# A mixer's first 60 microseconds: dt made token by token, two half projections ahead of the last norm tiles, identity transposes and a table load while inputs arrive

## The chip, the cores and the metric

The kernel runs on one core of a Trainium2 chip. A core has TensorE (PE, the matrix multiplier; its weight loads are shown apart as PEld), VectorE (DVE), ScalarE (ACT), GpSimd (POOL), a SyncE queue (SP) that issues DMAs, and on-chip memories: SBUF for operands, PSUM for what PE writes. The metric is device time in microseconds. The kernel before takes 2033.29 us (median of three executions, 2032.45 to 2035.05).

## The reference

The block reads 512 frames and 16 meta tokens of width 1024. It normalises every row, projects it to many columns, runs a chunked state-space scan and a short convolution, merges both, and ends with a large expert layer. Only its first part is touched by the change:

```python
h = jnp.concatenate([pad, meta, x], axis=1)
u = rmsnorm(h, ln_mix[l]) * valid
proj = u @ w_in[l]
z, xs, bs, cs, dt, sb, sc, sx, gates = jnp.split(proj, split_idx, axis=-1)
...
xbc = jax.nn.silu(causal_dwconv(xbc, conv_w) + conv_b) * valid
dt = jax.nn.softplus(dt.astype(jnp.float32) + dt_bias)      # 32 columns, one per head
a = -jnp.exp(a_log.astype(jnp.float32))
y = ssd_chunked_scan(xh * dtg[..., None], dtg * a, bs, cs)  # needs a running sum of dt * a
```

The width of `dt` is 32, one number per head and token. Every other slice of the projection is a multiple of 128 wide.

## The kernel before

**Number format.** Every matrix product that matters is made of three passes on PE: each operand is split into a rounded high part and the rest (`whi`, `wlo` of a weight; `uh`, `ul` of the normalised rows), and high x high, high x low and low x high are summed in PSUM. A weight block of 128 x 1024 is loaded by an SP DMA into `raw`, rounded by ACT into `whi` (L156), and DVE subtracts to get `wlo` (L157). A `Stream` object does this one block ahead of use; it has four `raw` buffers and three of each of `whi` and `wlo`.

**The norm.** Five tiles of rows enter: the 16 meta rows (`xm`) and four tiles of 128 frames (`xin`). They are handled in two groups, tiles 0 to 2 and tiles 3 and 4. Of each group ACT squares and sums the rows (L172; DVE for the 16 rows, L170), DVE computes the reciprocal root by three Newton steps (L128 to L133) and scales the rows into `xn` (L178). PE then transposes each tile, eight blocks of 128 columns in two PSUM banks (L187, tile `tps`); ACT rounds them into `uh` (L189) and DVE subtracts into `ul` (L190). From then on tokens run along the free axis: `uh` and `ul` hold 528 tokens.

**The projections.** `ft` (L224) makes one block of 128 output columns for all 528 tokens: 8 blocks of the inner dimension, 3 passes each, in two halves of 264 tokens, which is 48 passes with 264 moving columns (L233, tile `pj`, two PSUM buffers). The first block holds `dt`; it is called with `split=True`, so its first half (24 passes) needs the tokens of tiles 0 to 2 alone and stands ahead of the transposes of tiles 3 and 4. ACT copies the 32 useful rows out (L240), PE transposes them back to tokens-by-heads (L243, L245, tile `dtps`), and DVE and ACT make softplus from that (L246 to L266, `adt` at the end). Then come the blocks of group 0: `xs` twice, `bT` and `cT` by `ft`, each followed by a convolution and silu on ACT and DVE, then `zs` (tile `pz`).

**The running sums.** When `adt` is there, PE makes the running sums (L270 to L274: `meps`, `acps`, `atps`), short passes of 32 moving columns with a fixed 128 x 128 matrix on either side. They are in plain fp32, which costs two passes for each product. I call these 34 passes the burst. The scan of group 0 needs them.

**What sets the order.** The code is given to a scheduler that fixes the order of instructions on each engine when the kernel is built; on the chip every engine then runs its own list strictly in that order, and waits at an instruction until its inputs are there. After the first 60 us PE has a list of products up to the end of the kernel, with the other engines beside it.

## Time and profile before

| what | value |
|---|---|
| median of the runs | 2033.29 us |
| profiled execution | 2032.79 us, its span 2031.1 us |
| PE busy | 2001.7 us, 99% of the span |
| DVE, ACT, POOL busy | 1470.3, 914.8, 528.3 us |
| chain that ended last | PE 91%, DVE 6%, DMA 1%, ACT 1%, issue 1% |
| mean granted clock of TensorE | 0.997 of full speed |

A line of the timeline reads: start in us from the span's beginning, duration, engine, line of the kernel, operation, output<-inputs, shapes, count, and in brackets the idle time before it and who ended that. Consecutive instructions of one kind stand on one line with their count. A PE row's duration holds the time that a pass needs to run through the array, so the distance from one start to the next is what a pass costs in a dense row. [...]

### The profile page before, as it was taken

The page shows a single profiled execution, that of the slowest core. Times are in us where ns is not written, and L with a number is a line of the kernel's source. Part 1 is how long each engine was busy: PE and PEld are TensorE (multiplying, and loading weights), DVE is VectorE, ACT ScalarE, POOL GpSimd, SP SyncE. Part 2 cuts the span into 40 slices and gives each one's busy share as a digit, 9 for nine tenths or more (in the row PEclk, how much of TensorE's full clock was granted, in tenths as well). Part 3 has the DMA queues.
Part 4 walks back from the last instruction along what each step waited for, and adds up shares of the span by engine and source line. Part 5 has one row for each costly group of instructions (what it writes and reads, how often), then busy time and mean ns, then how long its engine had stood idle before and what let it go on. Part 6 is the DMA issues. An engine that isn't in the chain of part 4 may idle for free.

```text
span 2031.1 us, 31082 instructions
## 1 busy us (share of the span) xinstructions
PE 2001.7 (99%) x11944; PEld 1821.4 (90%) x11944; DVE 1470.3 (72%) x2705; ACT 914.8 (45%) x1281; POOL 528.3 (26%) x435
## 2 busy tenths in 40 slices
PE   7999999999999999999999999999999999999997
PEld 6999999999888888889999999999999998888886
DVE  6577777764322236479787879698988888988887
ACT  4877777732222223333447588433333332333333
POOL 1222222200000000331000000467555555633330
PEclk9999999999999999999999999999999999999999
DMA  4322323222222234224556667999999999999992
GB/s 150 121 95 89 100 87 96 84 74 94 94 94 94 96 112 166 73 84 143 183 178 219 244 242 275 372 396 397 396 396 353 359 352 334 392 380 382 385 379 101
DMA packets 175844, 439.57 MB, mean 216 GB/s; under 512 B 13776, under 2 KB 81584, under 8 KB 175568
## 3 DMA queue, kind: packets, MB, share of 16 engines
q1 hardware_dynamic: 135088, 290.62, 41.1%
q0 software_dynamic: 40320, 145.40, 19.3%
q8 instruction: 93, 1.52, 0.3%
q10 hardware_dynamic: 288, 1.57, 0.2%
q14 instruction: 55, 0.45, 0.1%
HBM read 395.53 MB, written 42.01 MB: 215 GB/s over the span
## 4 chain that ended last, share of the span: by engine, by line
PE 91%; DVE 6%; DMA 1%; ACT 1%; issue 1%; SPq 0%; POOL 0%; ACTq 0%; DVEq 0%; POOLq 0%
PE pj L233 13%; PE vps L137 8%; PE vps L136 8%; PE vps L138 8%; PE sps L136 7%; PE sps L137 7%; PE sps L138 7%; PE f L137 2%; PE f L136 2%; PE f L138 2%; PE gps L834 2%; PE pz L137 1%; PE pz L138 1%; PE pz L136 1%; PE qps L137 1%; PE qps L138 1%
## 5 line engine op out<-in xcount | busy, mean ns | idle before, releaser
L156 ACT CAST whi<-raw 128x1024 fp32r<-128x1024 f32 x393 | 411.9, 1050 | 811.9 <-issue 189.9
L157 DVE TENSOR_TENSOR wlo<-raw,whi 128x1024 fp32r<-128x1024 f32 x374 | 459.5, 1230 | 299.6 <-ACT whi L156 286.8
L136 PE MATMUL sps<-u2h,whi 128*128 128x384 f32 x1024 | 344.4, 336 | 0.0
L138 PE MATMUL sps<-u2h,wlo 128*128 128x384 f32 x1024 | 343.4, 335 | 0.3
L137 PE MATMUL sps<-u2l,whi 128*128 128x384 f32 x1024 | 342.9, 335 | 0.0
L137 PE MATMUL vps<-wlo,wh 128*128 128x512 f32 x768 | 299.3, 390 | 0.8 <-DVE wlo L157 0.8
L136 PE MATMUL vps<-whi,wh 128*128 128x512 f32 x768 | 299.0, 389 | 0.0
L138 PE MATMUL vps<-whi,wl 128*128 128x512 f32 x768 | 298.9, 389 | 0.0
L894 POOL DMA_INDIRECT row<-v,eix x128 | 180.1, 1407 | 213.6 <-DVE acc L906 194.4
L894 POOL DMA_INDIRECT row<-u,eix x128 | 190.9, 1491 | 131.1 <-DVE row L904 94.2
L136 PEld LDWEIGHTS sps<-u2h,whi 128*128 128x128 f32 x1024 | 192.3, 188 | 1.9
L137 PEld LDWEIGHTS sps<-u2l,whi 128*128 128x128 f32 x1024 | 192.3, 188 | 1.9
L138 PEld LDWEIGHTS sps<-u2h,wlo 128*128 128x128 f32 x1024 | 192.2, 188 | 1.6 <-DVE wlo L157 1.6
L138 PEld LDWEIGHTS vps<-whi,wl 128*128 128x128 f32 x768 | 144.1, 188 | 30.1
L137 PEld LDWEIGHTS vps<-wlo,wh 128*128 128x128 f32 x768 | 144.2, 188 | 29.5 <-DVE wlo L157 1.5
L136 PEld LDWEIGHTS vps<-whi,wh 128*128 128x128 f32 x768 | 144.1, 188 | 28.7 <-ACT whi L156 0.5
L233 PE MATMUL pj<-uh,whi 128*128 128x264 f32 (+1 forms) x784 | 165.4, 291 | 0.2 <-ACT uh L189 0.2
L906 DVE SCALAR_TENSOR_TENSOR acc<-row,sdot,acc 128x1024 f32<-128x1024 f32 x128 | 163.9, 1281 | 0.9
L233 PE MATMUL pj<-ul,whi 128*128 128x264 f32 (+1 forms) x784 | 162.2, 286 | 0.3 <-DVE ul L190 0.2
L233 PE MATMUL pj<-uh,wlo 128*128 128x264 f32 (+1 forms) x784 | 162.3, 286 | 0.0
L904 DVE SCALAR_TENSOR_TENSOR row<-row,u2t 128x1024 f32<-128x1024 f32 x128 | 151.3, 1220 | 12.3 <-DMA row<-u,eix 12.2
L999 ACT CAST wh<-wt 128x768 fp32r<-128x768 f32 x64 | 53.6, 838 | 163.2 <-PE vps L137 139.8
(286 smaller groups left out, 3610.5 us busy)
## 6 DMA issues: line engine op xcount, KB each, us to landing
raw<-u_t SPq DMA_DIRECT2D x128, 512.0 KB, 5.2
raw<-v SPq DMA_DIRECT2D x128, 512.0 KB, 12.3
raw<-w_a SPq DMA_DIRECT2D x73, 512.0 KB, 3.5
gsc<-gst SPq DMA_DIRECT2D x48, 512.0 KB, 4.4
gt<-gsc SPq DMA_DIRECT2D x32, 768.0 KB, 16.2
raw<-w_b SPq DMA_DIRECT2D x40, 512.0 KB, 3.4
asc<-so SPq DMA_DIRECT2D x36, 384.0 KB, 2.6
raw<-asc SPq DMA_DIRECT2D x36, 384.0 KB, 10.8
```

Of the source, the lines that this page charges most:

```text
L136: PE.matmul(ps, lh, rh, start=start, stop=False)
L137: PE.matmul(ps, lh, rl, start=False, stop=False)
L138: return PE.matmul(ps, ll, rh, start=False, stop=stop)
L156: A.copy(hi, r)
L157: self.last = self.lo(i).tensor_tensor(lo, r, hi.bitcast(F32), op=OP.subtract)
L233: PE.matmul(ps[:, hf, :w], w_[:, ks], u_[:, k, off + hf * w:off + (hf + 1) * w], start=(k == 0 and q == 0), stop=(k == KD - 1 and q == 2))
L834: PE.matmul(ps[:, i], oi[:, j, 1], og[:, j, x], start=x == 0, stop=x == 1)
L894: PL.indirect_dma_start(out=row, out_offset=None, in_=a["uv"[i // n]], in_offset=bass.IndirectOffsetOnAxis(ap=eix[:, i % n:i % n + 1], axi ...
L904: V.scalar_tensor_tensor(row, row, 1.0, u2t, op0=OP.mult, op1=OP.mult, accum_out=sdot[:, k])
L906: V.scalar_tensor_tensor(acc[:, 0], row, sdot[:, k], acc[:, 0], op0=OP.mult, op1=OP.add)
L999: A.copy(wh, wt)
```

## The change

Four things are edited, all within the first part of the program.

- A one-column `Square` on ACT is put ahead of everything, so that ACT loads its table before the inputs are there. The end of `norm_rows` (scale and add epsilon) moves into the loop, after the splitting of tile 2.
- 60 transposes of the identity matrix on PE into a scratch PSUM tile (`wm`) are put ahead of the first tile.
- `dt` is computed with the tokens as the stationary operand: for each of the five tiles of tokens, 8 blocks x 3 passes with `uh` or `ul` (16 or 128 tokens) as weights and the 32 useful columns of `whi` or `wlo` moving. The result is tokens-by-heads at once, so the copy L240 and the transposes L243 and L245 go. It makes 120 passes in place of 48 and 5 transposes. Tiles 0 to 2 are done ahead of tiles 3 and 4.
- The first halves of the next two projections (`xs` twice, 24 passes each) are issued between the two groups, so three weight blocks, not one, are loaded and split ahead of tiles 3 and 4.

```diff
+    warm = const.tile([P, 1], F32, name="warm")
+    A.activation(warm, ones[:, :1], AF.Square)
...
-    def norm_rows(pl, tiles, rows, ss):
+    def squares(pl, tiles, rows, ss):
...
-        n = max(rows)
-        V.tensor_scalar(ss[:n], ss[:n], 1.0 / D, EPS, op0=OP.mult, op1=OP.add)
...
+    def ft_open(off=0):
+        hi, lo = ws.q.pop(0) if ws.q and ws.i <= HELD else ws.next()
+        return psA.tile([P, 2, 512], F32, name="pj", tag="pj"), hi, lo, off
+
+    def ft_half(f, hs):
+        ps, hi, lo, off = f
+        w = (TW - off) // 2
+        for k in range(KD):
+            ks = slice(k * P, (k + 1) * P)
+            for q, (w_, u_) in enumerate(((hi, uh), (hi, ul), (lo, uh))):
+                for hf in hs:
+                    PE.matmul(ps[:, hf, :w], w_[:, ks], u_[:, k, off + hf * w:off + (hf + 1) * w],
+                              start=(k == 0 and q == 0), stop=(k == KD - 1 and q == 2))
+        return ps[:, :, :w]
+
+    begun = []
+
+    def ft(off=0):
+        if begun:
+            return ft_half(begun.pop(0), (1,))
+        return ft_half(ft_open(off), (0, 1))
...
+        wm = psA.tile([P, 4, P], F32, name="wm", tag="pj")
+        for i in range(WARM):
+            PE.transpose(wm[:, i % 4], ident, ident)
...
+        def dt(i, c0):
+            hi, lo = wdt
+            for k in range(KD):
+                sl, hs = slice(c0, c0 + rows[i]), slice(k * P, k * P + H)
+                mm3(dtps[:rows[i], i], uh[:, k, sl], ul[:, k, sl], hi[:, hs], lo[:, hs], k == 0, k == KD - 1)
...
+            squares(pi, [tiles[i] for i in b], [rows[i] for i in b], sq)
+            with ExitStack() as after:
+                if split:
+                    after.enter_context(tc.issue_after(split.ins))
+                V.tensor_scalar(sq, sq, 1.0 / D, EPS, op0=OP.mult, op1=OP.add)
+                rsqrt(pi, rs, sq)
...
+                if i == 2:
+                    ws.emit()
                 xn = scaled(pi, tiles[i], rows[i], rs[:rows[i], j:j + 1], lnb)
-                to_split_T(psB, (("tr", "st"), ("y", "yt"))[i % 2], xn, rows[i], uh, ul, c0)
+                split = to_split_T(psB, [("st", "y", "yt")[(2 * i + n) % 3] for n in range(2)], xn, rows[i], uh, ul, c0)
...
+            for i, c in zip(b, cs):
+                dt(i, c)
+            if not begun:
+                for _ in range(2):
+                    ws.emit()
+                    begun.append(ft_open())
+                    ft_half(begun[-1], (0,))
...
-        ps = ft(True)
-        dtf = pi.tile([H, TW], F32, name="dtf")
-        A.copy(dtf.rearrange("p (a b) -> p a b", a=2), ps[:H])
...
-        PE.transpose(ps[:NM, 0], dtf[:, :NM], ident[:H, :H])
-        for c in range(NT):
-            PE.transpose(ps[:, 1 + c], dtf[:, NM + c * P:NM + (c + 1) * P], ident[:H, :H])
```

How the built programs stand on an engine is shown here for three places. A row is a line of the kernel, the operation, output<-inputs, the output's shape and a count. `pj` is a projection's PSUM tile, `tps` that of the transposes, `dtps` that of dt, `whi` and `wlo` a weight block's parts.

On ACT at the start of the program, the kernel before:

```order
L172 ACT_TABLE_LOAD
L172 ACTIVATE junk,sq<-xin 128x1024 x3
L264 ACTIVATE alog<-alog 128x32
L172 ACTIVATE junk,sq<-xin 128x1024
L189 CAST uh<-tps 128x4x16 x2
L156 CAST whi<-raw 128x1024
L189 CAST uh<-tps 128x4x128
L156 CAST whi<-raw 128x1024
L189 CAST uh<-tps 128x4x128 x3
```

and the changed kernel at the same place:

```order
L89 ACT_TABLE_LOAD
L89 ACTIVATE warm<-ones 128x1
L178 ACTIVATE junk,sq<-xin 128x1024 x3
L300 ACTIVATE alog<-alog 128x32
L178 ACTIVATE junk,sq<-xin 128x1024
L162 CAST whi<-raw 128x1024 x3
L193 CAST uh<-tps 128x4x16 x2
L193 CAST uh<-tps 128x4x128 x8
```

Three roundings of weight blocks (`whi`) now stand ahead of the first rounding of transposed rows (`uh`); before, the first `uh` stood ahead of the first `whi` and the others were mixed.

On PE from the start of the program, the kernel before:

```order
L187 MATMUL tps<-ident,xn 128x16 x8
L187 MATMUL tps<-ident,xn 128x128 x16
L233 MATMUL pj<-uh,whi 128x264 x2
L233 MATMUL pj<-ul,whi 128x264
L233 MATMUL pj<-uh,wlo 128x264
```

and the changed kernel:

```order
L229 MATMUL wm<-ident 128x128 x60
L191 MATMUL tps<-ident,xn 128x16 x8
L191 MATMUL tps<-ident,xn 128x128 x4
L142 MATMUL dtps<-whi,uh 16x32
L143 MATMUL dtps<-wlo,uh 16x32
L191 MATMUL tps<-ident,xn 128x128 x12
L144 MATMUL dtps<-whi,ul 16x32
L142 MATMUL dtps<-whi,uh 16x32
```

Two passes of tile 0's dt now stand among the transposes of tile 1, ahead of twelve of them; the rest of dt for tiles 0 to 2 (16x32 and then 128x32 outputs, 70 more passes) follows, and then 48 passes `pj`.

On PE around the transposes of tiles 3 and 4, the kernel before:

```order
L233 MATMUL pj<-uh,wlo 128x264
L187 MATMUL tps<-ident,xn 128x128 x16
L233 MATMUL pj<-uh,whi 128x264 x2
L233 MATMUL pj<-ul,whi 128x264 x2
L233 MATMUL pj<-uh,wlo 128x264
```

and the changed kernel:

```order
L214 MATMUL pj<-uh,wlo 128x264
L191 MATMUL tps<-ident,xn 128x128 x12
L142 MATMUL dtps<-whi,uh 128x32
L143 MATMUL dtps<-wlo,uh 128x32
L191 MATMUL tps<-ident,xn 128x128 x4
L144 MATMUL dtps<-whi,ul 128x32
L142 MATMUL dtps<-whi,uh 128x32
L143 MATMUL dtps<-wlo,uh 128x32
```

After the transposes stood the second half of dt's block (24 passes of 264 columns); now 48 passes of 32 columns stand there, two of them ahead of the last four transposes, and then the second halves of the two `xs` blocks. The burst stood five passes before the end of the second `xs` block and now stands in the middle of `cT`'s.

## Rows read from the trace of the kernel before

**Rows 1.** The page: the span, the engines' busy times, and the engines' shares of the chain that ended last.

```profile
span 2031.1 us, 31082 instructions
PE 2001.7 (99%) x11944; PEld 1821.4 (90%) x11944; DVE 1470.3 (72%) x2705; ACT 914.8 (45%) x1281; POOL 528.3 (26%) x435
...
PE 91%; DVE 6%; DMA 1%; ACT 1%; issue 1%; SPq 0%; POOL 0%; ACTq 0%; DVEq 0%; POOLq 0%
```

**Rows 2.** PE in order of time, 12 to 28.4 us: start, duration, line, output<-inputs, shapes, count, idle time before and who ended it.

```profile
12.39 3.07 PE L187 MATMUL tps<-ident,xn 16*128 16x16 f32 x16 [12.39 <-DVE xn L178]
15.64 1.94 PE L187 MATMUL tps<-ident,xn 128*128 128x128 f32 x8 [0.17 <-DVE xn L178]
17.43 0.81 PE L233 MATMUL pj<-uh,whi 128*128 128x264 f32 x2
18.48 0.59 PE L233 MATMUL pj<-ul,whi 128*128 128x264 f32 x1 [0.24 <-DVE ul L190]
...
22.17 0.42 PE L233 MATMUL pj<-uh,wlo 128*128 128x264 f32 x1
22.39 0.32 PE L233 MATMUL pj<-uh,whi 128*128 128x264 f32 x1
...
24.74 2.26 PE L187 MATMUL tps<-ident,xn 128*128 128x128 f32 x16 [1.42 <-DVE xn L178]
27.23 0.51 PE L233 MATMUL pj<-uh,whi 128*128 128x264 f32 x2 [0.24 <-ACT uh L189]
```

**Rows 3.** POOL (one row, the identity matrix) and ACT in order of time, the first 16 us, the same columns.

```profile
1.20 0.28 POOL masks.py:199 TENSOR_SCALAR_AFFINE_SELECT ident<-ident 128x128 f32<-128x128 f32 x1
...
4.95 1.28 ACT L172 ACT_TABLE_LOAD   x1 [4.95 <-DMA xin<-x]
...
13.72 0.30 ACT L189 CAST uh<-tps 128x64 fp32r<-128x64 f32 x2
13.92 1.05 ACT L156 CAST whi<-raw 128x1024 fp32r<-128x1024 f32 x1
...
15.34 1.06 ACT L156 CAST whi<-raw 128x1024 fp32r<-128x1024 f32 x1
```

**Rows 4.** The first four loads of weight blocks, by the tile `raw` and the stretch 3.5 to 6 us in which they are issued: issue durations, first and last start, and time from issue to landing.

```profile
L153 SPq DMA_DIRECT2D raw<-w_a x4: 452/506/677, 3.8 to 5.4; - x4
...
DMA to landing us min/median/max: 10.0/11.2/12.2
```

**Rows 5.** DVE in order of time, 8 to 34 us.

```profile
13.95 0.35 DVE L190 TENSOR_TENSOR ul<-tps,uh 128x64 fp32r<-128x64 f32 x2 [0.50 <-ACT uh L189]
14.22 1.27 DVE L178 SCALAR_TENSOR_TENSOR xn<-xin,rs,lnb 128x1024 f32<-128x1024 f32 x1
15.41 1.21 DVE L157 TENSOR_TENSOR wlo<-raw,whi 128x1024 fp32r<-128x1024 f32 x1
16.55 2.47 DVE L190 TENSOR_TENSOR ul<-tps,uh 128x512 fp32r<-128x512 f32 x4
```

**Rows 6.** PE in order of time around the burst, 42.5 to 54 us.

```profile
42.54 0.41 PE L233 MATMUL pj<-uh,wlo 128*128 128x264 f32 x2
42.79 0.40 PE L233 MATMUL pj<-uh,whi 128*128 128x264 f32 x2
43.48 0.21 PE L270 MATMUL meps<-adt,stril 16*16 16x32 f32 x2 [0.29 <-DVE adt L266]
...
43.87 0.39 PE L273 MATMUL acps<-adt,stril 128*128 128x32 f32 x2
44.09 0.39 PE L273 MATMUL acps<-adt,ones 128*128 128x32 f32 x2
...
46.33 0.62 PE L273 MATMUL acps<-adt,ones 128*128 128x32 f32 x2
...
47.90 0.61 PE L273 MATMUL acps<-adt,stril 128*128 128x32 f32 x2
48.32 0.61 PE L273 MATMUL acps<-adt,ones 128*128 128x32 f32 x2
...
49.43 0.81 PE L233 MATMUL pj<-ul,whi 128*128 128x264 f32 x2
...
50.48 0.65 PE L233 MATMUL pj<-uh,whi 128*128 128x264 f32 x2
...
53.12 0.44 PE L233 MATMUL pj<-uh,whi 128*128 128x264 f32 x2
```

**Rows 7.** PE by stretches: the stretch, its length, PE's busy time and passes, the granted clock, DMA share and GB/s.

```profile
17.40:22.40 5.00, 4.76 (x21) 1.00 0.50 157
...
43.40:46.30 2.90, 2.82 (x22) 1.00 0.02 6
46.40:49.40 3.00, 3.00 (x13) 0.50 0.00 0
49.43:53.10 3.67, 3.67 (x17) 0.50 0.08 18
```

**Rows 8.** PE's weight loads of the burst by shape, 43.4 to 46.2 us: the shape of the stationary operand, count, busy us, mean ns of one.

```profile
L273 PEld LDWEIGHTS acps<-adt,stril 128*128 128x128 f32 x6 | 0.9, 192 | 0.0
...
L274 PEld LDWEIGHTS atps<-triu,adt 128*32 128x32 f32 x4 | 0.3, 107 | 0.1
L270 PEld LDWEIGHTS meps<-adt,stril 16*16 16x16 f32 x2 | 0.1, 88 | 0.5 <-issue 0.5
```

## The prediction

> **What bounds the kernel now.** I read the page first: PE is busy 99% of the span and makes up 91% of the chain that ended last [rows 1]. So the end moves by what PE loses or wins, and only where PE waits or runs at a low clock is there something to win. Then I read PE in order of time over the start, and ACT, DVE and the loads beside it. [...] It does nothing before 12.39 us. It has done no more than 24 projection passes when the transposes of tiles 3 and 4 begin at 24.74, after a wait of 1.42 us. [...] From there PE is dense, with one exception, the burst. The clock fell at 46.33, 2.9 us after the burst had begun, while PE issued without a pause, and came back at 53.12, 3.7 us after wide passes had begun again [rows 6]; the granted clock is 0.50 in both stretches between [rows 7]. In the first rise, 3.9 us of wide passes came before it (18.48 to 22.39) [rows 2]. So in this kernel narrow passes cost PE its clock, and the change adds 120 narrow passes.

> **A point to compare at.** I take the moment at which PE has finished dt and both `xs` blocks, without the burst. Before, the last `xs` pass ends at 50.48, where `bT` begins. The burst took 43.03 (42.79 and two passes) to 49.43, 6.4 us, and made the last four passes 0.1 us dearer each [rows 6]: 50.5 - 6.4 - 0.4 = 43.7 us. The burst stays in both kernels and I give it the same price in both.

> **The table load.** It stood for 1.28 us between the first tile's landing and its squares [rows 3], and goes into the wait for inputs. DVE can start its roots that much earlier. I count nothing for it, because what opens PE's work is now something else (next part); it costs at most nothing and wins at most 1.28 us.

> **The start.** PE's first dt pass needs `uh` of tile 0. Before, ACT rounded that at 13.72, ahead of the first weight block [rows 3]. Now three weight blocks stand ahead of it on ACT. Their loads are issued from 3.8 to 5.4 us and land 10.0 to 12.2 us later [rows 4], so the first is there at 13.9, the fourth at 17.6, and the third, 1.25 us apart, at about 16.4. ACT ends its rounding (1.05 us) at 17.4, and `uh` of tile 0 is there at about 17.6. On DVE two blocks of `wlo` (1.21 us each) stand ahead of `xn` of tile 2 (1.27) and of `ul` of tile 0 [rows 5]: 16.2 when the second `whi` is there, then 17.4, 18.7 and 18.9. Twelve transposes wait behind the two first dt passes for banks that `ul` of tile 0 sets free, and start at 18.9. PE has been nearly idle from the end of the 60 transposes to there, so I take the low clock: eight transposes took 1.94 us with the last one's 0.42 in it [rows 2], 0.22 each and 2.5 for twelve: 21.4. Before, the same tiles were transposed at 17.4.

> **The 60 transposes.** They start when the identity is there, at about 1.5 us [rows 3]. At 0.22 each they end at 14.5, at 0.11 at 8. Both are ahead of 17.6, so by themselves they cost nothing. Do they raise the clock? The rows don't settle it: eight transposes on end before 17.43 didn't, and sixteen from 24.74, with 1.42 us of idle ahead of them, didn't let it fall [rows 2]. But what they raise is lost again: from their end to 18.9 PE has four transposes of tile 1 and some 16-column passes to do, far less than the burst, in which the clock fell [rows 6]. So in the sum they win nothing. [...] No row here shows a long run of transposes from the low clock. [...]

> **dt by tokens.** 24 passes have a stationary operand of 16 columns, 96 one of 128, and all move 32 columns. The burst's passes are the nearest rows: 128 stationary, 32 moving, two in 0.22 us at the fast clock (43.87 to 44.09) and two in 0.42 at the slow one (47.90 to 48.32) [rows 6], that is 0.11 and 0.21. They are bound by the weight load, which takes 192 ns with 128 columns, 107 with 32 and 88 with 16 [rows 8]; dt's operand has the same four bytes. Of 16 columns I take 0.06 at the slow clock, between 0.03 (from the 0.1 us that the load is shorter) and 0.21. Before, dt took 48 wide passes, 5.8 us at the fast clock; now the 96 alone take 10.6. Tile 0: 24 x 0.06 = 1.4, to 22.8. Tiles 1 and 2: 48 x 0.21 = 10.1, to 32.9. DVE has their `ul` ready by about 22.5 (four pieces of 0.6 and a `wlo` of 1.2 after 18.9 [rows 5]), so PE is what is late.

> **First halves.** 48 wide passes, the clock low for the first 3.8 us as in both rises: 17 x 0.22 + 31 x 0.12 = 7.5, to 40.4.

> **Tiles 3 and 4.** Their `xn` is ready long before. From the first transpose to the first pass that used them took 2.5 us (24.74 to 27.23 [rows 2]): 42.9. Then 48 narrow passes; the clock falls 2.9 us in, as in the burst: 26 x 0.11 + 22 x 0.21 = 7.5, to 50.4. Second halves again 7.5: 57.9.

> **The sum.** 57.9 - 43.7 = 14.2 us later. The profiled execution took 2032.79 (the span of 2031.1 [rows 1] and 1.7 around it, which stays), so the change gives 2047.0; the median before, 2033.29, is 0.5 higher, and I don't correct for that. I add nothing for waits behind it, where three things are priced at zero. The chain from dt to `adt` starts later, and the burst now stands in the middle of `cT`; it waited 0.29 us for `adt` before [rows 6], and with more convolution steps between on DVE it could wait 0 to 2. ACT's exponentials for the scan come later against PE: 0 to 2. And the burst may meet the clock at another moment: its 6.4 us would be 4.5 at the fast clock, and the passes behind it lose 1.7 (17 x 0.1), so it may give back 3.6 or cost 2 more.

> **Rivals.**
> - *Narrow passes don't let the clock fall, but don't raise it either.* dt's operands are not plain fp32, and its rounded format may count otherwise than the burst did. Up to 42.9 all is as above; then 48 x 0.11 and 48 x 0.12 give 54.0, 10.3 later: 2043.1. Against it: the burst's passes have the same shapes.
> - *The fast clock holds from the 60 transposes on.* Then transposes from 18.9 take 1.3, tile 0 0.7, tiles 1 and 2 5.3, halves 5.8, transposes 2.5, dt 5.3, halves 5.8: 45.6, 1.9 later: 2034.7, which can't be told from no change. For it: the clock outlived 23.1 to 27.2 with little work [rows 2]. Against it: 46.33.
> - *Faster: a narrow pass isn't bound by its load.* Two of the three passes of a block share their stationary operand; if PE kept it, or pulled loads ahead, and the clock held as well, a pass could cost 0.03 as with 16 columns: 96 x 0.08 = 7.7 less than the case above, 5.8 us gained: 2027.0. It decides from a pass of about 0.05 on. Against it: in 43.87 to 44.09 the loads were not hidden.
> - *The clock stays low through all of it.* Both pairs of halves at 0.22 (10.6) and dt at 0.21 (10.1) from 32.9 on, transposes 4: 68, 24 later: 2057.

> **How the numbers follow.** The forecast 0.60, the first rival 0.15, the second 0.13, the third 0.07, the fourth 0.05. A measurement here can tell 0.2%, 4.1 us. The third rival is faster: 0.07. The second is the same: 0.13. The others are slower: 0.80. The forecast's own range is 2042 to 2052, from the 3.6 given back and the 4 of waits; the range that holds the time 8 times in 10 goes down to the second rival, 2034, and up to 2053.

> **What would show it.** Passes of `dtps` 0.21 us apart for tiles 1 and 2, and the first half of `xs` starting near 33 us; a recorded rise near 37, a fall between 45 and 50, another rise before 56. ACT's first `uh` after 17 us. `bT` beginning near 58 with no burst before it. Wrong it would be if `dtps` passes start 0.11 apart throughout, or if the granted clock shows no fall before the burst: then the second rival holds. If they start closer than 0.1, the third.

## The result and the profile after

The changed kernel took 2046.1 us (median of 6 runs, 2043.57 to 2049.5) against 2032.99 of the kernel before on the same chips (6 runs, 2031.56 to 2035.8): a ratio of 1.0063, 95% interval 1.0049 to 1.0076. A ratio is worked out from all executions of both kernels, so it needn't be the quotient of the two medians. Two executions far off the others, one of before (5148.99 us) and one of `table_alone` (2475.86 us), are left out of every time and ratio below. The change is slower, by 13 us where 14 had been forecast. The profiled execution took 2044.01 us, among the fastest of the six, so its trace shows the mild form of the loss: 11.2 us on the span of before.

The page's first two lines answer to [rows 1]. PE has 127 more instructions and 16.5 us more busy time, and the share stays at 99%.

```profile
span 2042.3 us, 31329 instructions
PE 2018.2 (99%) x12071; PEld 1837.4 (90%) x12071; DVE 1472.0 (72%) x2705; ACT 913.3 (45%) x1279; POOL 534.6 (26%) x435
```

PE by stretches, with the columns of [rows 7]: stretch, length, busy time and passes, granted clock, DMA share, GB/s. The limits stand where the clock changes or where one kind of pass ends.

```profile
1.54:5.10 3.56, 3.56 (x17) 1.00 0.79 262
5.20:10.00 4.80, 4.80 (x45) 1.00 0.99 274
...
17.90:22.20 4.30, 3.24 (x28) 0.50 0.72 226
22.30:25.60 3.30, 3.30 (x40) 1.00 0.40 146
25.70:29.70 4.00, 4.00 (x20) 0.50 0.00 0
29.75:32.40 2.65, 2.65 (x13) 0.50 0.00 0
32.50:36.80 4.30, 4.30 (x37) 1.00 0.00 0
38.10:42.65 4.55, 4.22 (x40) 1.00 0.00 0
42.75:45.90 3.15, 3.15 (x17) 0.50 0.00 0
45.95:49.50 3.55, 3.55 (x17) 0.50 0.08 10
49.60:53.45 3.85, 3.85 (x33) 1.00 0.35 127
62.60:66.55 3.95, 3.91 (x30) 1.00 0.38 133
66.65:70.00 3.35, 3.35 (x16) 0.50 0.08 20
```

Before, the clock fell once at the start, in the burst. Now it falls in the middle of dt for tiles 1 and 2 (25.65), again in dt for tiles 3 and 4 (42.7), and once more in the burst (66.6); each time it is wide passes of the projections after which it comes back (32.5, 49.5, 70.0). It had also fallen at 15.4, while PE was nearly idle (busy for 1.38 of the 5.40 us from 10.0 on), and come back at 22.2 behind twelve transposes and most of tile 0's narrow passes. The first two rows are the 60 transposes: the clock reads 1.00 in both because no change is on record before 5.17, but 17 passes in 3.56 us are 0.21 apart and 45 in 4.80 are 0.107 apart, so 5.17 is a rise. The first row of [rows 7] prints 1.00 for the same reason: before, passes of 264 columns are 0.22 us apart up to 22.39 (22.17 to 22.39 [rows 2]) and 0.12 later (two in 0.25, 42.54 to 42.79 [rows 6]), so the change that comes first on record is a rise there as well.

PE in order of time, with the columns of [rows 2]. Tile 0's narrow passes, one of which waits for `uh`; the twelve transposes; then the two kinds of narrow pass on either side of the fall; then the first wide one.

```profile
1.54 8.52 PE L229 MATMUL wm<-ident 128*128 128x128 f32 x60 [1.54 <-POOL ident masks.py:199]
...
17.91 0.21 PE L142 MATMUL dtps<-whi,uh 128*16 128x32 f32 x1 [4.77 <-ACT uh L193]
17.95 0.19 PE L143 MATMUL dtps<-wlo,uh 128*16 128x32 f32 x1
19.20 2.79 PE L191 MATMUL tps<-ident,xn 128*128 128x128 f32 x12 [1.06 <-DVE ul L194]
21.64 0.37 PE L144 MATMUL dtps<-whi,ul 128*16 128x32 f32 x1
...
22.41 0.26 PE L142 MATMUL dtps<-whi,uh 128*128 128x32 f32 x1
22.52 0.26 PE L143 MATMUL dtps<-wlo,uh 128*128 128x32 f32 x1
...
25.87 0.38 PE L142 MATMUL dtps<-whi,uh 128*128 128x32 f32 x1
26.08 0.37 PE L143 MATMUL dtps<-wlo,uh 128*128 128x32 f32 x1
...
29.71 0.57 PE L214 MATMUL pj<-uh,whi 128*128 128x264 f32 x1
...
53.36 0.28 PE L214 MATMUL pj<-uh,wlo 128*128 128x264 f32 x1
53.48 0.41 PE L214 MATMUL pj<-uh,whi 128*128 128x264 f32 x2
...
62.64 0.21 PE L306 MATMUL meps<-adt,stril 16*16 16x32 f32 x2 [0.38 <-DVE adt L302]
...
71.86 0.29 PE L142 MATMUL pz<-whi,uh 128*128 128x256 f32 x1
```

Passes with 128 stationary columns start 0.11 us apart up to 25.65 and 0.21 apart from there on (25.87 to 26.08): the prices of the burst [rows 6]. `bT` begins at 53.48, where the forecast said 57.9. Before, it began at 42.79: from there on PE has two passes of 264 columns ahead of the burst and 46 behind it, up to the first of 258 columns, with which `cT` begins. Those 48 are one block. In before's rows, `cT` and then `pz`:

```profile
56.79 0.40 PE L233 MATMUL pj<-uh,whi 128*128 128x258 f32 x2
...
62.56 0.29 PE L136 MATMUL pz<-whi,uh 128*128 128x256 f32 x1
```

So the burst of before stood two passes into `bT`, and not five passes ahead of the end of the second `xs` block, as the part on the change has it; the point to compare at is 42.8 and not 43.7. The change is 10.7 us late there. Most of it is kept: the first pass of `pz` is at 71.86 against 62.56, 9.3 later, and `f`, the next stage, begins at 414.31 against 405.26, 9.05 later. The last 2.1 us of the 11.2 come much later, from a cause of their own (the runs on the table load, below).

The waits ahead of the start are the ones forecast. ACT in order of time, to compare with [rows 3]:

```profile
14.13 1.04 ACT L162 CAST whi<-raw 128x1024 fp32r<-128x1024 f32 x1
15.42 1.04 ACT L162 CAST whi<-raw 128x1024 fp32r<-128x1024 f32 x1 [0.25 <-DMA raw<-w_a]
16.70 1.04 ACT L162 CAST whi<-raw 128x1024 fp32r<-128x1024 f32 x1 [0.23 <-DMA raw<-w_a]
17.65 0.81 ACT L193 CAST uh<-tps 128x64 fp32r<-128x64 f32 x3
```

### The profile page after: what moved, and what is told of

Same layout as the page of the kernel before. It is cut to its first block, busy times and chain, and to the rows that moved or that the text cites. A ratio compares the mean times of both kernels' runs of the same rounds, so it can differ in the third digit from the quotient of the medians.

```text
span 2042.3 us, 31329 instructions
## 1 busy us (share of the span) xinstructions
PE 2018.2 (99%) x12071; PEld 1837.4 (90%) x12071; DVE 1472.0 (72%) x2705; ACT 913.3 (45%) x1279; POOL 534.6 (26%) x435
## 4 chain that ended last, share of the span: by engine, by line
PE 91%; DVE 5%; DMA 1%; ACT 1%; issue 1%; SPq 0%; POOL 0%; ACTq 0%; DVEq 0%; POOLq 0%
PE pj L214 13%; PE vps L143 8%; PE vps L144 8%; PE vps L142 8%; PE sps L142 7%; PE sps L144 7%; PE sps L143 7%; PE f L143 2%; PE f L142 2%; PE f L144 2%; PE gps L870 2%; PE pz L143 1%; PE pz L144 1%; PE pz L142 1%; PE qps L144 1%; PE qps L143 1%
## 5 line engine op out<-in xcount | busy, mean ns | idle before, releaser
L930 POOL DMA_INDIRECT row<-u,eix x128 | 200.2, 1564 | 123.4 <-DVE row L940 85.1
```

Of the source, the lines that this page charges most:

```text
L930: PL.indirect_dma_start(out=row, out_offset=None, in_=a["uv"[i // n]], in_offset=bass.IndirectOffsetOnAxis(ap=eix[:, i % n:i % n + 1], axi ...
```

## The experiments

All edits are to the changed kernel unless another is named. The theory was that the loss is dt by tokens: its load-bound narrow passes, and the clock that they let fall. The rivals were the later `uh` (three weight blocks ahead of it on ACT), the transposes, and the late part.

**dt in wide passes again.** dt has its 32 heads on the stationary side and 264 token columns moving, in two halves of 24 passes; all other edits stay.

```diff
+                    PE.matmul(ps, w_[:, hs], u_[:, k, sl], start=(k == 0 and q == 0), stop=(k == KD - 1 and q == 2))
...
-            for i, c in zip(b, cs):
-                dt(i, c)
+            dt(0 if not begun else 1)
```

> dt is made as before, with heads out and 264 tokens moving (48 wide passes in two halves, 5 transposes at the end); the 60 transposes, the table load, the order on ACT and the two early half projections stay as in the changed kernel. My theory: dt and both xs blocks are done near 44 us without the running sums, as before, so 2032 to 2036, 10 to 14 us below the changed kernel, and no fall of the clock between the first halves and the running sums. Rival (three weight blocks ahead of uh on ACT, a late start, are the main cost): 2042 or later.

2033.16 us (10 runs) against 2032.77, ratio 1.0004 (0.9994 to 1.0013). The loss goes with dt by tokens. What the other edits leave are two small parts that cancel: in the traced execution `f` begins at 403.68, 1.6 us ahead of before, and the late part (the runs on the table load, below) costs 2.0. From 22.7 us on, the stretches show no fall up to the end of the burst; it comes at 60.2, right behind it:

```profile
22.70:37.00 14.30, 13.59 (x113) 1.00 0.06 23
37.00:60.10 23.10, 22.88 (x187) 1.00 0.33 107
```

**No transposes**, and **96 moving columns.** The first leaves out the 60 unread transposes. The second moves 96 columns in each dt pass; 64 of them are computed and not used.

```diff
-        wm = psA.tile([P, 4, P], F32, name="wm", tag="pj")
-        for i in range(WARM):
-            PE.transpose(wm[:, i % 4], ident, ident)
```

```diff
-                sl, hs = slice(c0, c0 + rows[i]), slice(k * P, k * P + H)
+                sl, hs = slice(c0, c0 + rows[i]), slice(k * P, k * P + 96)
...
```

> The 60 identity transposes are left out; with them gone the built program also has the first roundings of uh ahead of two of the three weight blocks on ACT, as before the change. My theory (narrow dt passes are slow and cost the clock): PE's first long stretch starts some 3 us earlier, but at the low clock throughout dt of tiles 1 and 2 (0.21 us a pass); against the changed kernel (2046.1) 0 to 4 us less, 2042 to 2046. Rival (the transposes keep the clock up for what follows and so pay): 3 us or more above the changed kernel, 2049 or later. Rival (the late uh on ACT is the main cost of the change): 8 us or more below it, 2038 or less.

> Each dt pass moves 96 columns of the weight block in place of 32 (the 64 others are computed and not used); number of passes, weight loads and everything else stay. My theory (the clock falls because the passes move so little): still about 0.11 us a pass at the fast clock, no fall of the granted clock before the running sums, and although PE does three times the work the kernel gets faster than the changed one by 4 to 8 us, 2038 to 2042. Rival (the number of passes alone costs, whatever they move): 2046, the granted clock as in the changed kernel. Rival (a pass of 96 columns is no longer bound by its load): 0.16 us or more a pass, 2046 to 2052.

2043.34 us (4 runs, ratio 1.0056, 1.0039 to 1.0073) and 2045.1 (4 runs: three from 2045.07 to 2045.4, one 2039.62; 1.0055, 1.0038 to 1.0071). Without the transposes the kernel isn't slower, so in this kernel they win nothing; the two edits can't be told apart quite, since without them the engines' order comes out otherwise too (PE's first dt pass starts at 15.59 for 17.91). The second missed: I had expected three times the columns to hold the clock, and in three runs of four the time stays where it was. The run of 2039.62, at a mean clock of 0.994 for 0.991 to 0.992 of the others, lies in the range of my theory, and has no trace. In the traced one the passes of tiles 1 to 4 stay 0.11 us apart at the high clock, so they cost no more than narrow ones, but the clock falls in them just the same, at 44.4 and, here, at 27.3:

```profile
27.22 0.29 PE L144 MATMUL dtps<-whi,ul 128*128 128x96 f32 x1
27.33 0.40 PE L142 MATMUL dtps<-whi,uh 128*128 128x96 f32 x1
27.53 0.41 PE L143 MATMUL dtps<-wlo,uh 128*128 128x96 f32 x1
```

**`uh` first.** ACT rounds weight blocks 1 and 2 behind the last `uh` of tile 2.

```diff
...
-                    ws.emit()
+                    with tc.issue_after(rounded[0].ins):
+                        ws.emit()
```

> Only the order on ACT is changed: the rounding of weight blocks 1 and 2 is put behind the last uh of tile 2. My theory: the twelve transposes behind tile 0's first dt passes start some 1.5 us earlier, and that is all: 2043.5 to 2046. Rival (the late uh is the main cost of the change): 2038 or less.

2048.89 us (4 runs, ratio 1.0078, 1.0061 to 1.0095). A miss: I had given it 2043.5 to 2046. The transposes did start at 18.00 and not 19.20, and still the kernel got no faster. What the 1.2 us bought was lost to the clock: in the profiled execution it didn't rise before 37.3, so all of dt for tiles 1 and 2 and more than half of the first halves went at the low level.

```profile
20.50:31.20 10.70, 10.70 (x71) 0.50 0.30 98
31.30:37.30 6.00, 6.00 (x28) 0.50 0.00 0
```

**No early table load**, and **the table load alone.** The trace of after had shown 2.1 us that arise between 1290 and 1700 us. The early load writes a tile of 4 bytes per partition in the pool that lives as long as the kernel. One run takes load and tile out of after, the other adds them, and nothing else, to before.

```diff
-    warm = const.tile([P, 1], F32, name="warm")
-    A.activation(warm, ones[:, :1], AF.Square)
```

> After, without the table load while inputs arrive and without the 4-byte tile that it writes. Theory for the start: the load costs nothing there; without it ScalarE loads its table ahead of the first square, which goes at most 1.3 us later, and the first pz stands within 2 us of 71.86. Theory for a late part: every changed kernel run so far loses another 2.1 us against before between 1290 and 1700 us, at an even rate, in the passes vps<-whi,wl and wlo,wh (231 and 229.5 ns apart on average against 227.5 before), whatever it does at the start; what they share is this small tile, which moves all later tiles' places by 4 bytes. If the place is the cause, the late part is gone here: 2042 to 2045 us, last vps minus first vps as in before (732.2 us against 734.3). Rival (the late part comes from the other edits, such as the names and order of the first tiles): it stays, 2044 to 2049.

> Before, with nothing but the table load while inputs arrive and its 4-byte tile added. If the tile's place is the cause of the late 2.1 us, this kernel has it: the distance from first to last vps is 734.3 us and not 732.2, and the time is 2033 to 2036 us against 2032.8, less whatever the earlier table gives at the start (first pz 0 to 1.3 us ahead of 62.56). Rival (the place doesn't matter): 732.2 us from first to last vps, and 2031 to 2033.

2044.46 us (4 runs, ratio 1.0059, 1.0043 to 1.0075) and 2034.22 (9 runs, ratio 1.0006, 0.9996 to 1.0016). The times alone would settle nothing; the traces do. PE's groups of 1330 to 1690 us by shape (count, busy us, mean ns of one, idle), first before, then after:

```profile
L137 PE MATMUL vps<-wlo,wh 128*128 128x512 f32 x264 | 103.0, 390 | 0.0
L138 PE MATMUL vps<-whi,wl 128*128 128x512 f32 x264 | 102.8, 390 | 0.0
```

```profile
L143 PE MATMUL vps<-wlo,wh 128*128 128x512 f32 x261 | 102.3, 392 | 0.0
L144 PE MATMUL vps<-whi,wl 128*128 128x512 f32 x260 | 102.1, 393 | 0.0
```

Then after without the tile, and before with it:

```profile
L141 PE MATMUL vps<-wlo,wh 128*128 128x512 f32 x260 | 101.4, 390 | 0.0
L142 PE MATMUL vps<-whi,wl 128*128 128x512 f32 x260 | 101.3, 389 | 0.0
```

```profile
L141 PE MATMUL vps<-whi,wl 128*128 128x512 f32 x262 | 102.9, 393 | 0.0
L140 PE MATMUL vps<-wlo,wh 128*128 128x512 f32 x262 | 102.7, 392 | 0.0
```

The 2 to 3 ns, which are means, follow the tile. Counted from pass to pass, the same 1740 passes of this stage take 341.51 to 341.53 us in all seven traces without the tile in that pool and 343.15 in all seven with it, and the rest of the stage 377.3 against 377.6: 2.0 us. PE never waits in it, so it is the pass itself that is longer. I read no addresses; that the tile shifts the place of what is allocated behind it, and that this is what these passes feel, is the reading that fits, not one that was shown. At the start the load of `table_alone` has the first `pz` at 61.77 for 62.56: 0.8 us won, within the 0 to 1.28 of the forecast. In the changed kernel the load won nothing: without it ACT's first `uh` stands at 17.66 for 17.65. `no_early_table` did miss what I gave its start, a first `pz` within 2 us of 71.86; it is at 75.93, because the clock there stayed low up to 38.1 (table in the next part).

**The tile moved.** `dt_wide_again` with the table load kept, and its tile in the first stage's pool, which is given back.

```diff
-    warm = const.tile([P, 1], F32, name="warm")
+    warm = pi.tile([P, 1], F32, name="warm")
```

> The kernel dt_wide_again (all of the change but dt by tokens), with the 4-byte tile of the table load put in the pool of the first stage, which is freed after it. By the theory of the place the late 2.1 us go and the 1.5 us that dt_wide_again is ahead at the start (first f 403.68 against 405.26) come out: 2030 to 2032 us, 1 to 2 us under before. Rival (place doesn't matter): 2033 as dt_wide_again.

2030.4 us (11 runs) against 2032.86, ratio 0.9991 (0.9982 to 1.0). Load kept, tile elsewhere: the late part is gone, so it isn't the load.

**Narrow and wide in turns.** Each narrow pass of tiles 1 to 4 is followed by a wide pass of the half projections; as many of each as in after.

```diff
+        def turns(narrow, wide):
+            for _ in narrow:
+                next(wide, None)
...
+            turns((p for i, c in zip(b, cs) if i for p in dt(i, c)),
+                  (p for f in begun for p in ft_passes(f, (0 if first else 1,))))
```

> After, but the narrow passes of dt for tiles 1 to 4 take turns on TensorE with the 264-column passes of the half projections (one narrow, one wide), 48 and 48 in either block; the number of passes of each kind stays. Theory (most of the loss beyond the pass count is the clock, which falls because narrow passes stand in a row): with a wide pass after every narrow one the clock rises once near 22 to 24 us and doesn't fall before the running sums; a block of 96 passes at 0.11 us takes 10.6 us where the changed kernel's profile has 14.3 (22.41 to 36.73) and 14.1 (39.27 to 53.36), so the time is 2037 to 2041 us against 2046.1, with the first pz 5 to 8 us ahead of 71.86. Rival (any load-bound narrow passes among them let the clock fall, as with 96 columns): two falls before the running sums remain and the time stays at 2043 to 2049. Second rival (changing tiles pass by pass costs of itself): the clock holds but the passes take more than 0.13 us apart.

2039.37 us (6 runs; five from 2038.85 to 2040.82, one 2048.1), ratio 1.0043 (1.0028 to 1.0059). As the theory had it: the same passes in another order are 6.7 us cheaper by the medians (4.5 between the traced executions, 4.0 of them up to `f`), and in the profiled execution the clock holds from 23.8 to behind the first burst passes. The pass itself is no cheaper: a pair takes 0.235 us, twice a pass of 128 stationary columns at the high clock (0.11). The sign I gave for `pz` can't be read, as it stands ahead of the burst here (59.61) and behind it in after.

```profile
23.90:59.50 35.60, 35.27 (x300) 1.00 0.14 47
```

```profile
24.91 0.18 PE L244 MATMUL dtps<-wlo,uh 128*128 128x32 f32 x1
24.94 0.37 PE L214 MATMUL pj<-ul,whi 128*128 128x264 f32 x1
25.14 0.18 PE L244 MATMUL dtps<-whi,ul 128*128 128x32 f32 x1
```

**More transposes, and the order.** `wide_tile_moved` with 36 more unread transposes in PE's idle time behind tile 0's; with `uh` first; and with both (30 transposes).

```diff
+                if i == 0:
+                    for w in range(36):
+                        PE.transpose(wm[:, w % 4], ident, ident)
```

> wide_tile_moved with 36 more of the same unread transposes on TensorE behind tile 0's eight (its idle time from 13.0 to 19.2 us there, in which the clock fell at 13.48). Theory (transposes count for the clock here, since the first 60 raised it at 6.65): the clock doesn't fall before 20 us; the 12 transposes of 19.17 to 21.75 take 1.3 us less, the ten passes from 21.8 to 23.7 some 1.0 us less, so 2027.5 to 2028.7 us against 2030.4. Rival (transposes don't count for the clock; the first rise had another cause): the clock falls near 13.5 and rises near 23.7 all the same, and the time stays at 2030 to 2031.

> wide_tile_moved with the edit of uh_first: ScalarE rounds two blocks of weights behind the last uh of tile 2 and not ahead of the first uh. Theory: the 12 transposes start 1.2 us earlier (18.0 for 19.17); as there are no narrow passes here that the clock falls in, what lies before the rise near 23.7 us goes at the low clock, so half or more of it stays: 2029.2 to 2030.0 us. Rival (this order is harmful of itself, as uh_first was 2.8 us slower than after): 2031 to 2034.

> Both edits at once, with 30 more transposes for 36. Theory: the clock is held and the chain from the first uh is 1.2 us earlier, so 2026.3 to 2027.8 us. Rival (then the second block of weights is late for the half projections, by up to 2.5 us of ScalarE and VectorE work that now stands behind): 2027.8 to 2030.

Against 2033.18: 2031.45 us (ratio 0.9992, 0.9983 to 1.0001), 2030.25 (0.9987, 0.9978 to 0.9996), 2029.76 (0.9990, 0.9981 to 0.9999), 11 runs each. The transposes held the clock: in the profiled execution of `wide_fill` it is high from 7.3 to 20.9, where `wide_tile_moved` was low from 13.5 to 23.7. But the price I gave that was wrong: it fell at 20.95, after PE had waited 2.3 and 0.7 us for buffers, and cost the first dt passes what the transposes had won. The order is harmless in this kernel, 0.2 us above the top of what I gave it, so `uh_first` wasn't slow by its order as such; what its trace shows in its place is the narrow passes at the low clock. With both edits the clock stays up from 7.2 to 58.3, the end of the burst, and still the time misses the 2026.3 to 2027.8 of the theory. It lies in the range of the rival, but the wait for the second weight block that the rival names isn't in the trace: from 17.7 to 30 us PE waits only for `ul` and `uh` (1.75, 0.29 and 0.53 us).

```profile
7.20:58.30 51.10, 47.17 (x389) 1.00 0.43 148
```

These three and `wide_tile_moved` are all faster than the changed kernel. Against before they lie some 0.1% lower; the intervals of `wide_order` and `wide_fill_order` end just below 1 (0.9996, 0.9999), those of the other two at 1.0 and 1.0001. Between the four the runs don't choose.

**In turns, with the clock held.** `turns` with the tile moved and the 36 transposes.

> The kernel turns (dt by tokens, its narrow passes taking turns with wide ones) with the 4-byte tile in the first stage's pool and the 36 more transposes: dt by tokens with the clock held and nothing lost late. It prices the narrow passes by their number alone, against wide_fill: 96 passes at 0.117 us and 24 at 0.03 make 11.9 us, against 48 wide ones at 0.12 and 5 transposes at 0.12, 6.4 us. Theory: 5 to 6 us over wide_fill, 2033 to 2034.5, 5 to 6 us under turns (2039.37; 2.1 of them the tile's). Rival (with the clock held a narrow pass costs no more than its share of a wide one): within 2 us of wide_fill.

2043.41 us (6 runs, ratio 1.0056, 1.0034 to 1.0077): a miss as a time. The six runs are three from 2037.02 to 2039.35 with a mean granted clock of 0.996 to 0.997, and three from 2047.47 to 2049.24 with 0.990 to 0.991. The profiled one is of the first kind, and its clock was high through all of dt:

```profile
4.40:62.30 57.90, 52.68 (x467) 1.00 0.41 138
```

There both `xs` blocks are done at 46.3, against 43.6 in `wide_fill`, which lost about 1.7 of its own to the clock (3.4 us at half speed): narrow passes cost some 4 us by their number alone. The theory's 5 to 6 is met only at `f` (408.92 against 403.13), where a fall behind the burst, from 62.3 to 69.1, is in it. Of the second kind there is no trace. Its mean clock gives an estimate of what it lost: the low level counts half (a granted clock of 0.50), so 0.006 less over 2040 us is 24 us more at that level, in which 12 us are lost; the middle runs of the two kinds (2037.72 and 2048.9) are 11.2 apart. Where those 24 us lie isn't shown. So with turns the clock held in the traced executions, and it seems not to hold in every one.

## Why the prediction was right, and where its sum was off

The cause was right: dt by tokens carries the loss (`dt_wide_again`), by passes bound by the weight load, and by the clock that they let fall (`turns`: same passes, 6.7 us less). That it is the load is a reading that fits: at the high clock passes with 128 stationary columns are 0.11 us apart with 32 moving columns as with 96 (`dt_96_columns`), and those with 16 stationary columns 0.026. That the time came out so near, 2047.0 for 2046.1, is partly luck: it rests on errors of opposite sign, and the median lies between two ways in which the clock can go. The steps, by the ends of each; the column on the right is the profiled execution of `no_early_table` (2045.67 us), whose PE does the same from 17.9 us on:

| step | forecast | after | `no_early_table` |
|---|---|---|---|
| twelve transposes start | 18.9 | 19.20 | 19.21 |
| ... end | 21.4 | 21.64 | 21.65 |
| dt of tile 0 | 22.8 | 22.41 | 22.43 |
| dt of tiles 1 and 2 | 32.9 | 29.71 | 32.67 |
| first halves | 40.4 | 36.85 | 41.02 |
| dt of tiles 3 and 4 | 50.4 | 45.94 | 48.76 |
| second halves | 57.9 | 53.48 | 56.03 |

- *The point to compare at* was misread by 0.9 us: 42.8, where `bT` begins, and not 43.7 (section on the result). By its own terms the forecast should have been 15.1 us and not 14.2, and each rival comes 0.9 later against before.
- *The start and the table load* hold within 0.3 us.
- *Tile 0's dt* was mis-sized: 0.026 us a pass at the low clock, just under the lower bound I had (0.03), where I took 0.06. From the end of the transposes it took 0.8 us for 1.4.
- *Tiles 1 and 2* is the term that failed in this execution: "48 x 0.21 = 10.1". It measured 7.3 (29 passes at 0.11, 19 at 0.21), because the clock rose at 22.23, before the first of them. I had the clock low until wide passes began. In `no_early_table`, and in `uh_first`, it was low, and the term was 10.2 us:

```profile
22.43 0.37 PE L140 MATMUL dtps<-whi,uh 128*128 128x32 f32 x1
22.64 0.37 PE L141 MATMUL dtps<-wlo,uh 128*128 128x32 f32 x1
...
32.45 0.37 PE L142 MATMUL dtps<-whi,ul 128*128 128x32 f32 x1
32.67 0.57 PE L212 MATMUL pj<-uh,whi 128*128 128x264 f32 x1
```

- So the same passes met the clock in two ways. By the signs that I had named (the halves near 33, a rise near 37, a fall between 45 and 50), the execution of `no_early_table` is the forecast one (32.67, 38.1, 48.4), and the traced one of after isn't. The runs of after fit two ways as well: three from 2043.57 to 2044.57 at mean clocks of 0.991 to 0.993, three from 2047.63 to 2049.5 at 0.990 to 0.991. That the clock makes this spread is a reading that fits; the slower three have no trace. (A mean clock counts what lies before the first recorded change as 1.00, so it doesn't compare between kernels: `no_transposes` has 0.996, though its passes are 0.21 apart up to 32.4.) Why the clock rises at 22 in one execution and at 38 in another I can't say from these runs.
- *Tiles 3 and 4* took 9.1 us, transposes included, for 10.0; the second halves 7.5, as forecast; the first halves 7.1 for 7.5. Their passes are 0.22 us apart at the low clock (30.07 to 30.29) and 0.12 at the high one (32.49 to 32.61), as priced.
- *What I priced at nothing behind it* came to -1.4 up to the first `pz` (18.4 us from the start of `bT`, 19.8 before): the burst waited 0.38 us for `adt`, and the low clock that it brought lasted 3.4 us (66.6 to 70.0) where before it lasted 6.8.
- *What I left out* is the tile: 2.0 us late in the kernel. I had taken the table load for an edit at the start only. Where the forecast had 14.2 us at the start and none late, this execution has 9.1 and 2.1.
- *The transposes.* I left their effect on the clock undecided and said that it would be lost again. They raised it: with nothing but transposes on PE their distance went from 0.21 to 0.107 us at 5.17, and `wide_fill` held the clock with more of them (high from 7.3 to 20.9). In after it was lost at 15.4.
- *The rivals.* The second, fast clock throughout, came about in one execution, that of `turns_fill`, and there, with the passes in another order, took 46.3 to this point for the 45.6 that I gave it; so its sum was sound, and in after its condition wasn't met. The third is refuted: in a row, narrow passes of 128 stationary columns start 0.11 apart and no less. Of the first, one half is seen: where the clock was low, 48 narrow passes didn't raise it (`no_early_table`), but where it was high they let it fall. The fourth, the low clock all through, is in no trace.

## What to carry to other kernels

A change that kept the arithmetic and made each pass narrower paid twice on TensorE here: by the number of passes, which with 128 stationary columns cost 0.11 us each at the high clock, with 32 moving columns as with 96, and by the clock, which at 32 and at 96 columns fell while PE had no gap at all (25.65 in after, 27.3 in `dt_96_columns`). Such a term had two values (7.3 us in after, 10.2 in `no_early_table`, for dt of tiles 1 and 2), so price it at both levels, and look at the granted clock of each execution before you explain a spread. Put narrow passes among wide ones if they must be (`turns`: 6.7 us less than after by the medians), and keep the small tiles of a start out of a pool that lives to the end (2.0 us here), or compare a late, even stage pass by pass.
